# Delta net on unscaled queries and keys, decay sums spread by DMA, and two token chunks that enter the mixers with their norm's factor

## The chip, the core and the metric

The program runs on one core of a Trainium2 chip. A core has a matrix engine (TensorE, PE in the profile; PEld is its weight load), a vector engine (VectorE, DVE), a scalar engine (ScalarE, ACT), GpSimd (POOL) and SyncE (SP), whose queue issues nearly every DMA of this kernel. The metric is the device time of one execution in microseconds (us). Lines such as L1001 are lines of the kernel before, unless the text says that they belong to the changed one.

## The reference, cut to what matters

One decoder layer: a feed-forward block, two mixers side by side (windowed attention and a gated delta net), and a second feed-forward block. 1024 prompt tokens and 64 sample tokens (8 sequences of 8) go through it together. The change lies in the norm ahead of the mixers and in the delta net.

```python
h = rms_norm(x, mix_norm_pre)            # x * rsqrt(mean(x*x) + 1e-6) * gain
qa, ka, va, qkvb, zb, ab, bb, ga, gb = split_columns(h @ w_in)
xb = silu(causal_conv(qkvb));  qb, kb, vb = split(xb)
qb = l2_normalize(qb) * 128 ** -0.5      # x * rsqrt(sum(x*x) + 1e-6)
kb = l2_normalize(kb)
g = -exp(a_log) * softplus(ab + dt_bias);  beta = sigmoid(bb)
# per head and chunk of tokens, in float32
gc = cumsum(g);  decay = exp(gc_i - gc_j) for j <= i
m  = strict_lower(beta * (k @ k.T) * decay)
k_cum, v_u = solve(I + m, [beta * k * exp(gc), beta * v])
v_new = v_u - k_cum @ S
o     = (q * exp(gc)) @ S + ((q @ k.T) * decay) @ v_new
S     = S * exp(gc_last) + (k * exp(gc_last - gc)).T @ v_new
ob = rms_norm(o, dn_out_norm) * silu(zb)
merged = sigmoid(ga) * (oa @ w_branch_a) + sigmoid(gb) * (ob @ w_branch_b)
```

A query's length scales its whole row of `o`, and the norm on `o` takes it out again but for the small constant under the root. The final states do not depend on the queries.

## The kernel before

**Layout.** Features lie on the 128 partitions and tokens along the free axis. The 1088 tokens are three chunks, `CH` = 0 to 384, 384 to 768 and 768 to 1088. A weight or activation is kept as two tiles, a rounded one and the remainder (`split`, `split_w`), and each product is three matrix products with a rounded float32 type (L138 to L140 in `gemm`, L343 to L345 in the down projection, L462 to L464 in the up projection of chunks 0 and 1). Products of the delta net and the sums over partitions are plain float32; the profile holds two records for each such product.

**Stages.** The first feed-forward block ends with `close1(c)` for each chunk: `post` (norm of the output, residual), then `make_xn` (L198, L199), which multiplies by the gain alone and splits, and `rms`, which makes the row factor `r2[c]` from a sum over partitions (L175, a product with a matrix of ones). For chunks 0 and 1 these generators are stepped while the block's last passes run (`take(late, 3)`, L627). The mixers take `xn2`; since the factor is not in it, every product's result is multiplied by `r2[c]` as VectorE copies it out of PSUM (L666, L683, L694, L957, L1018, L1031). Those results rotate through three PSUM buffers, `pa`.

**Mixers.** Keys, values and queries of the attention, then 16 attention items, the sample attention, four delta heads, and as filler the products of the convolution inputs (`conv_unit`), the z gates (`z_unit`) and 16 gate units (`gate_unit`, L1021 on), which hang on nothing but `xn2` and weights.

**A delta head** (`delta_head`) works in eight slots of 128 x 1088 each; heads 0 and 2 use one set, 1 and 3 the other, and small PSUM tiles come from `ph` or `py`. `l2` normalizes q and k: square, sum over partitions by a product with ones (L1001), root on ScalarE (L1002, L1003), one Newton step (L145, L146), scaling (L1008). L1060 and L1099 make the rows of the cumulated decay, the same on all partitions, by a product of a broadcast column with a triangle. L1063 is k against q, L1066 the decay's exponent, L1076 the decay into q on POOL, L1080 a transpose, L1083 k against k, L1135 the transposes of k and v, L1141 to L1152 a forward substitution in blocks of 32, L1165 and L1166 the scaling of the inverse by the columns `bg` and `bh`, L1217 to L1236 the walk over the chunks. At the end `colsum_rsqrt` does the output's norm, and the gate z comes back by DMA (L1275).

**What sets the order.** A scheduler orders each engine's instructions before the run by its own cost model; the program's order and `high_priority` are its input. On the chip every engine's queue runs in that order.

Of the kernel before, what the change touches and what calls it, by code (L numbers as in the profile page):

```python
# [7 lines left out]
F32 = mybir.dt.float32  # L8
# [27 lines left out]
def body(ctx: ExitStack, tc: tile.TileContext, d):  # L36
# [25 lines left out]
    gd = dp.tile([16, P, NT], F32, tag="gd", name="gd")  # L62

# [468 lines left out]
    hn2 = cp.tile([P, KT], F32, tag="hn2", name="hn2")  # L532
    nc.vector.tensor_scalar_mul(hn1, vec[:, V_N1A : V_N1A + KT], -0.5)
# [14 lines left out]
    with tc.tile_pool(name="f1", bufs=12, side="left", reuse_waits="tile") as big1, tc.tile_pool(  # L548
# [78 lines left out]
        f1.run(xs1, cx1, lambda: again(d["x2"], hn1, r1[2]), before, lambda g, i: (g, i) != (CUT, 0) and take(late, 3), r=lambda g: None if g else r1[2], first=first)  # L627
# [26 lines left out]

    def do_ab(c):
        a, b = CH[c]
        n = b - a
        ps = pa()
        xh, xl = xn2[c]
        for k in range(KT):  # L660
            for j in (0, 1) if k < KT - 1 else (1, 0):
                m, x = ((16, xh), (8, xl))[j]
                nc.tensor.matmul(ps[:m, :n], wab[:, k, :m], at(x, k), start=k + j == 0, stop=k - j == KT - 1)
        ab = t1()
        with tc.high_priority(offset=20000):
            nc.vector.scalar_tensor_tensor(  # L666
                out=ab[:16, :n], in0=ps[:16, :n], scalar=-0.5, in1=r2[c][:16, :], op0=ALU.mult, op1=ALU.mult
            )
        pst = pb()
        for o in range(a, b, P):  # L670
            w = min(P, b - o)
            i = o // P
            tk2 = pst[:w, i * 16 : i * 16 + 16]
            nc.tensor.transpose(tk2, ab[:16, o - a : o - a + w], ident[:16, :16])
            nc.vector.tensor_copy(atok[:w, i, :], tk2[:, 0:8])
            nc.vector.tensor_tensor(out=atok[:w, i, :], in0=atok[:w, i, :], in1=tk2[:, 8:16], op=ALU.add)

    def do_kv(dst, w, c):
        a, b = CH[c]
        ps = pa()  # L680
        mm = gemm(ps, w, xn2, c)
        with tc.high_priority(offset=20000):
            nc.vector.scalar_tensor_tensor(  # L683
                out=dst[:, a:b], in0=ps[:, : b - a], scalar=-0.5, in1=r2[c], op0=ALU.mult, op1=ALU.mult
            )
        return mm

    def do_q(t, w, c):
        a, b = CH[c]
        ps = pa()  # L690
        mm = gemm(ps, w, xn2, c)
        e = min(b, NPR)
        with tc.high_priority(offset=20000):
            nc.vector.scalar_tensor_tensor(  # L694
                out=YA[t][:, a:e], in0=ps[:, : e - a], scalar=-0.0625, in1=r2[c][:, : e - a], op0=ALU.mult, op1=ALU.mult
            )
# [81 lines left out]
    nc.vector.tensor_tensor(out=tk["bg"], in0=tk["bg"], in1=tk["beta"], op=ALU.mult)  # L778

# [166 lines left out]
    def conv_unit(u, dst):  # L946
        w = unit(U_QKV + u, f"qkv{u}")
        cw = [vec[:, V_CW + u * 4 + j : V_CW + u * 4 + j + 1] for j in range(4)]
        for c, (a, b) in enumerate(CH):
# [6 lines left out]
            with tc.high_priority(offset=20000):  # L956
                nc.vector.scalar_tensor_tensor(  # L957
                    out=pre[:, 3 : 3 + m], in0=ps[:, :m], scalar=-0.5, in1=r2[c][:, :m], op0=ALU.mult, op1=ALU.mult
                )
# [37 lines left out]
    def colsum_rsqrt(src, sq, ve, rr, tmp, scale, ps):  # L997
        nc.scalar.activation(sq, src, AF.Square)
        for a, b in ((0, 512), (512, 1024), (1024, NT)):
            pq = ps()  # L1000
            nc.tensor.matmul(pq[:, : b - a], ones, sq[:, a:b], start=True, stop=True)  # L1001
            nc.scalar.activation(ve[:, a:b], pq[:, : b - a], AF.Identity, scale=scale, bias=epsc)  # L1002
        nc.scalar.activation(rr, ve, AF.Abs_reciprocal_sqrt)  # L1003
        newton(rr, ve, tmp)

    def l2(x, A, l2s, ps):
        colsum_rsqrt(x, A[4], A[3], A[5], A[4], 0.25, ps)
        nc.vector.scalar_tensor_tensor(out=x, in0=x, scalar=-0.25 * l2s, in1=A[5], op0=ALU.mult, op1=ALU.mult)  # L1008

    def z_unit(h):  # L1010
        w = unit(U_Z + h, f"z{h}")
        for c, (a, b) in enumerate(CH):
            n = b - a
            ps = pa()
            gemm(ps, w, xn2, c)
            z = t1()
            with tc.high_priority(offset=20000):
                nc.vector.scalar_tensor_tensor(out=z[:, :n], in0=ps[:, :n], scalar=-0.5, in1=r2[c], op0=ALU.mult, op1=ALU.mult)  # L1018
            sg = t3()
            nc.scalar.activation(sg[:, :n], z[:, :n], AF.Tanh, scale=0.5)  # L1020
            nc.vector.scalar_tensor_tensor(out=z[:, :n], in0=sg[:, :n], scalar=1.0, in1=z[:, :n], op0=ALU.add, op1=ALU.mult)  # L1021
            nc.sync.dma_start(zd[h, :, a:b], z[:, :n])

    def gate_do(i, w, c):
# [4 lines left out]
        z = t1()  # L1029
        with tc.high_priority(offset=20000):  # L1030
            nc.vector.scalar_tensor_tensor(out=z[:, :n], in0=ps[:, :n], scalar=-0.5, in1=r2[c], op0=ALU.mult, op1=ALU.mult)  # L1031
            nc.scalar.activation(z[:, :n], z[:, :n], AF.Tanh, scale=0.5)
# [7 lines left out]
    def delta_head(h, A, ps):  # L1040
        q, k, v, M, L, U, QK, R = A
        ar = R[:, :NPR].rearrange("p (i c) -> p i c", c=P)
        mq = s2b.tile([P, 2 * NSM], F32, tag="mq", name=f"mq{h}", bufs=2)

# [9 lines left out]
        D, E = R[:, 0:512], R[:, 512:1024]  # L1054
        for c0 in (0, 4):
            pr, pq = ps(), ps()
            for i in range(4):
                w, cs, ix = tile_of(c0 + i)
                ps_i = slice(i * P, i * P + P)
                nc.tensor.matmul(pr[:, ps_i], tk["g"][:, ix : ix + 1].to_broadcast([P, P]), cst[:, C_TRI : C_TRI + P], start=True, stop=True)  # L1060
            for i in range(4):
                w, cs, ix = tile_of(c0 + i)
                nc.tensor.matmul(pq[:, i * P : i * P + P], k[:, cs], q[:, cs], start=True, stop=True)  # L1063
            for i in range(4):
# [3 lines left out]
                    in0=pr[:, i * P : i * P + P],  # L1068
# [5 lines left out]
            nc.scalar.activation(E, pr, AF.Exp)  # L1074
# [6 lines left out]
            for i in range(4):  # L1081
                w, cs, ix = tile_of(c0 + i)
                nc.tensor.matmul(pk[:, i * P : i * P + P], k[:, cs], k[:, cs], start=True, stop=True)  # L1083
            nc.scalar.copy(D, pt)
            for i in range(4):
# [4 lines left out]
                    scalar=tk["beta"][:, ix : ix + 1],  # L1090
# [4 lines left out]
        for c in range(8, 9):  # L1095
            w, cs, ix = tile_of(c)
            tri, neg = cst[:w, C_TRIS : C_TRIS + w], cst[:w, C_NEGS : C_NEGS + w]
            p = ps()
            nc.tensor.matmul(p[:, 0:w], tk["g"][:w, ix : ix + 1].to_broadcast([w, P]), tri, start=True, stop=True)  # L1099
            nc.tensor.matmul(p[:w, 128 : 128 + w], k[:, cs], k[:, cs], start=True, stop=True)  # L1100
            nc.tensor.matmul(p[:w, 256 : 256 + w], k[:, cs], q[:, cs], start=True, stop=True)
            Ds = ar[:w, 0, :w]
            nc.vector.scalar_tensor_tensor(
                out=Ds, in0=p[:w, 0:w], scalar=tk["gc"][:w, ix : ix + 1], in1=neg, op0=ALU.subtract, op1=ALU.add
# [3 lines left out]
            nc.scalar.activation(eR, p[:, 0:w], AF.Exp)  # L1108
# [6 lines left out]
                out=M[:w, cs], in0=p[:w, 128 : 128 + w], scalar=tk["beta"][:w, ix : ix + 1], in1=DT, op0=ALU.mult, op1=ALU.mult  # L1115
# [15 lines left out]
        for c0 in (0, 4):  # L1131
            for t in (k, v):
                p = ps()
                for i in range(4):
                    nc.tensor.transpose(p[:, i * P : i * P + P], t[:, (c0 + i) * P : (c0 + i + 1) * P], ident)  # L1135
                nc.scalar.copy(wide(t, c0), p)
# [26 lines left out]
        def scale_u(c, Ub):  # L1163
            w, cs, ix = tile_of(c)
            nc.vector.tensor_scalar_mul(Ub, U[:w, cs], tk["bg"][:w, ix : ix + 1])  # L1165
            nc.scalar.mul(U[:w, cs], U[:w, cs], tk["bh"][:w, ix : ix + 1])  # L1166
# [35 lines left out]
        nc.tensor.transpose(p[:w, 0:128], k[:, cs], ident)  # L1202
        nc.tensor.transpose(p[:w, 128:256], v[:, cs], ident)
        nc.scalar.copy(ar[:w, 6:8, :], p[:w, 0:256].rearrange("p (i c) -> p i c", c=P))
# [3 lines left out]
        nc.tensor.matmul(p5[:, :w], ar[:w, 6, :], Ub, start=True, stop=True)  # L1208
# [51 lines left out]
        for hf in range(2):  # L1260
# [8 lines left out]
            nc.tensor.matmul(p6, ar[:NSM, 6, :], vm, start=True, stop=True)  # L1269
# [6 lines left out]
        colsum_rsqrt(QK, q, k, v, M, 1.0 / P, ps)  # L1276
# [230 lines left out]
```

## Time and profile before

| | us |
|---|---|
| median of 3 runs (2459.77 to 2460.8) | 2460.74 |
| the profiled execution | 2454.17 |
| its span, from the first to the last instruction | 2452.4 |
| PE busy in the span | 2396.3 |
| DVE busy | 1752.0 |
| ACT busy | 1146.2 |

The mean granted clock of TensorE was 0.991. The first feed-forward block runs to about 760 us, its end and the first mixer products lie between 760 and 800, attention from 858 to 985, the delta heads from about 985 to 1460, the last gates to 1490, and then the branch projections, the output projection and the second feed-forward block. A row of a view by line reads: line, engine, operation, tiles written and read, shape, count, then busy time in us, mean ns of one, and the engine's idle time just before them with what ended it. A row by stretch of time gives each engine's busy time in it, the count of instructions, the granted clock, the busy share of the DMA engines and GB/s.

### The profile page before, as it was taken

How to read it: one execution, taken by the hardware profiler on the slowest of the kernel's cores; microseconds unless marked ns; L12 is line 12 of the kernel's file. 1: busy time of each engine (PE TensorE's matmuls, PEld its weight loads, DVE VectorE, ACT ScalarE, POOL GpSimd, SP SyncE). 2: the span in 40 equal slices, each digit the busy share in tenths (PEclk: the TensorE clock that was granted, in tenths of full speed). 3: DMA queues.
4: the chain of work that ended last, by engine and by line, in shares of the span. 5: the costliest groups of instructions: out<-in, count | busy, mean ns of one | idle time of the engine just before them, and what ended most of it. 6: DMA issues, size and time to landing. Idle time of an engine off the chain costs nothing.

```text
span 2452.4 us, 39218 instructions
## 1 busy us (share of the span) xinstructions
PE 2396.3 (98%) x14654; PEld 2307.2 (94%) x14654; DVE 1752.0 (71%) x3550; ACT 1146.2 (47%) x2326; POOL 48.6 (2%) x36
## 2 busy tenths in 40 slices
PE   8999999999999999999999999999999999999997
PEld 7999999999998988798898889999999999999997
DVE  8887657757788577698796646655997576676677
ACT  7644423324465377644655333255754333233344
POOL 0000000000000000000101000000000000000000
PEclk9999999999999999999999999999999999999998
DMA  7332212213454301222222345435523122122453
GB/s 269 125 112 86 74 48 86 70 52 112 155 175 142 105 29 45 77 65 73 71 68 73 99 143 158 142 129 184 182 93 97 48 82 78 45 85 80 152 164 133
DMA packets 159759, 257.98 MB, mean 105 GB/s; under 512 B 34800, under 2 KB 65968, under 8 KB 159560
## 3 DMA queue, kind: packets, MB, share of 16 engines
q1 hardware_dynamic: 159568, 255.47, 32.4%
q8 instruction: 115, 1.88, 0.3%
q14 instruction: 76, 0.62, 0.1%
HBM read 219.43 MB, written 36.96 MB: 105 GB/s over the span
## 4 chain that ended last, share of the span: by engine, by line
PE 43%; DVE 6%; DMA 2%; ACT 1%; issue 1%; SPq 0%; DVEq 0%; ACTq 0%
PE pa L139 6%; PE pa L140 6%; PE pa L138 6%; PE pa L462 4%; PE pa L463 4%; PE pa L464 4%; PE py L344 2%; PE py L345 2%; PE ph L345 2%; PE ph L344 2%; PE ph L343 2%; PE py L343 2%; DMA q_c_a<-in_up_dram 1%; DVE s L1149 1%; DVE s L1143 1%
## 5 line engine op out<-in xcount | busy, mean ns | idle before, releaser
L463 PE MATMUL pa<-cl,h_c_s 128*128 128x384 f32 x704 | 236.4, 336 | 4.7 <-DVE cl L272 4.7
L462 PE MATMUL pa<-ch,h_c_s 128*128 128x384 f32 x704 | 237.4, 337 | 2.0 <-DVE t L468 1.4
L464 PE MATMUL pa<-ch,l_c_s 128*128 128x384 f32 x704 | 236.2, 336 | 0.0
L468 DVE TENSOR_TENSOR t<-pa,t 128x384 f32<-128x384 f32 x308 | 170.3, 554 | 83.6 <-PE pa L464 83.1
L462 PE MATMUL pa<-ch,h_c_a 128*128 128x384 f32 x528 | 176.8, 335 | 0.1
L464 PE MATMUL pa<-ch,l_c_a 128*128 128x384 f32 x528 | 176.6, 334 | 0.0
L463 PE MATMUL pa<-cl,h_c_a 128*128 128x384 f32 x528 | 176.5, 334 | 0.0
L111 ACT CAST h_c_a<-r_c_a 128x512 fp32r<-128x512 f32 x132 | 81.8, 619 | 129.8 <-PE pa L463 110.9
L462 PEld LDWEIGHTS pa<-ch,h_c_s 128*128 128x128 f32 x704 | 132.8, 189 | 5.6 <-DVE t L468 5.2
L463 PEld LDWEIGHTS pa<-cl,h_c_s 128*128 128x128 f32 x704 | 133.0, 189 | 4.9 <-DVE cl L272 4.9
L464 PEld LDWEIGHTS pa<-ch,l_c_s 128*128 128x128 f32 x704 | 132.9, 189 | 0.0
L111 ACT CAST h_c_s<-q_c_s 128x512 fp32r<-128x512 f32 x132 | 82.0, 621 | 107.1 <-PE pa L463 96.3
L139 PE MATMUL pa<-xbl,h_ga 128*128 128x384 f32 (+1 forms) x384 | 129.3, 337 | 0.0
L138 PE MATMUL pa<-xbh,h_ga 128*128 128x384 f32 (+1 forms) x384 | 128.7, 335 | 0.0
L140 PE MATMUL pa<-xbh,l_ga 128*128 128x384 f32 (+1 forms) x384 | 128.4, 334 | 0.0
L462 PEld LDWEIGHTS pa<-ch,h_c_a 128*128 128x128 f32 x528 | 99.1, 188 | 0.8 <-DVE t L468 0.6
L463 PEld LDWEIGHTS pa<-cl,h_c_a 128*128 128x128 f32 x528 | 99.1, 188 | 0.0
L464 PEld LDWEIGHTS pa<-ch,l_c_a 128*128 128x128 f32 x528 | 99.1, 188 | 0.0
L138 PE MATMUL pa<-xbh,h_qkv 128*128 128x384 f32 (+1 forms) x288 | 96.7, 336 | 0.0
L139 PE MATMUL pa<-xbl,h_qkv 128*128 128x384 f32 (+1 forms) x288 | 96.6, 335 | 0.0
L140 PE MATMUL pa<-xbh,l_qkv 128*128 128x384 f32 (+1 forms) x288 | 96.3, 334 | 0.0
L111 ACT CAST h_c_s<-r_c_s 128x512 fp32r<-128x512 f32 x44 | 27.4, 623 | 146.4 <-PE pa L463 130.6
(603 smaller groups left out, 7438.4 us busy)
## 6 DMA issues: line engine op xcount, KB each, us to landing
r_c_a<-in_up_dram SPq DMA_DIRECT2D x132, 256.0 KB
q_c_a<-in_up_dram SPq DMA_DIRECT2D x44, 256.0 KB
q_ub<-in_up_dram SPq DMA_DIRECT2D x44, 256.0 KB
r_ub<-in_up_dram SPq DMA_DIRECT2D x44, 256.0 KB
r_ua<-in_up_dram SPq DMA_DIRECT2D x42, 256.0 KB
q_ua<-in_up_dram SPq DMA_DIRECT2D x42, 256.0 KB
r_da<-in_dn_dram SPq DMA_DIRECT2D x40, 256.0 KB
q_da<-in_dn_dram SPq DMA_DIRECT2D x40, 256.0 KB
```

Source lines behind the costliest of these rows:

```text
L111: nc.scalar.copy(hi, full)
L138: nc.tensor.matmul(ps[:, :n], hi[:, j, :], at(xh, k), start=first, stop=False)
L139: nc.tensor.matmul(ps[:, :n], hi[:, j, :], at(xl, k), start=False, stop=False)
L140: mm = nc.tensor.matmul(ps[:, :n], lo[:, j, :], at(xh, k), start=False, stop=last)
L343: nc.tensor.matmul(ps[:, :n], hi[:, i, :], hh, start=i == 0, stop=False)
L344: nc.tensor.matmul(ps[:, :n], hi[:, i, :], hl, start=False, stop=False)
L345: nc.tensor.matmul(ps[:, :n], lo[:, i, :], hh, start=False, stop=i == len(hs) - 1)
L462: nc.tensor.matmul(ps, wh[:, k, :], xh[:, k, :], start=k == 0, stop=False)
L463: nc.tensor.matmul(ps, wh[:, k, :], xl[:, k, :], start=False, stop=False)
L464: nc.tensor.matmul(ps, wl[:, k, :], xh[:, k, :], start=False, stop=k == 3)
L468: nc.vector.tensor_tensor(out=out, in0=ps, in1=other, op=ALU.add)
L1143: nc.vector.tensor_tensor(out=tv, in0=Md[:, j + 1 :, j : j + 1].to_broadcast([34, m, j + 1]), in1=Ld[:, j : j + 1, 0 : j + 1].to_broadcast ...
```

## The change

1. **The norm's factor.** For chunks 0 and 1 `rms` comes before the split, and `make_xnr` multiplies gain and row factor into the activations (changed lines 213, then 193 and 194 for the split). Chunk 2 stays as it was. The mixers' results of chunks 0 and 1 are then copied out of PSUM by ScalarE (`normed`), or, in the gates, read from PSUM by the tanh itself; chunk 2 still goes through VectorE. The generators are stepped four at a time instead of three.
2. **Unscaled q and k.** `l2` is gone. The keys are transposed to token rows at the head's start (changed line 1075), the transposed rows are squared and summed along the free axis on ScalarE and VectorE, and the factor, now one number per token in a column, goes into `beta`, `bg` and `bh`. The queries stay as the convolution left them; their squares are kept in HBM (`sqd`) and added under the root of the output's norm.
3. **Decay sums.** One transpose of `gc` and nine small DMAs put the cumulated decay in HBM (`gcd`); each head reads its row back to all 128 partitions with one DMA into the slot of `QK`, in place of L1060 and L1099.

```diff
     def close1(c):
             ...
-            yield from make_xn(y, xn2[c], V_MXA)
+            r2[c] = rtile("r2", c)
             spill(y, xd[c])
-            r2[c] = rtile("r2", c)
-            yield from rms(big1, lambda k: at(y, k), width(c), r2[c], 1.0 / 1024.0)
+            if c == 2:
+                yield from make_xn(y, xn2[c], V_MXA)
+                yield from rms(big1, lambda k: at(y, k), width(c), r2[c], 1.0 / 1024.0)
+            else:
+                yield from rms(big1, lambda k: at(y, k), width(c), r2[c], 1.0 / 1024.0)
+                yield from make_xnr(y, xn2[c], hnx, r2[c], c)
...
-        ... and take(late, 3), r=lambda g: None if g else r1[2], first=first)
+        ... and take(late, 4), r=lambda g: None if g else r1[2], first=first)
...
+    def normed(out, ps, c, scale=1.0, p=P, o=0):
+        n = out.shape[-1]
+        with tc.high_priority(offset=20000):
+            if c < 2:
+                nc.scalar.mul(out, ps[:p, o : o + n], scale)
+            else:
+                nc.vector.scalar_tensor_tensor(
+                    out=out, in0=ps[:p, o : o + n], scalar=-0.5 * scale, in1=r2[c][:p, o : o + n], op0=ALU.mult, op1=ALU.mult
+                )
...
+    psc = pb()
+    nc.tensor.transpose(psc[:36, :P], tk["gc"], ident)
+    gct = s2b.tile([36, P], F32, tag="gct", name="gct")
+    nc.vector.tensor_copy(gct, psc[:36, :P])
+    for c in range(9):
+        nc.sync.dma_start(gcd[:, c, :], gct[4 * c : 4 * c + 4, :])
...
     def gate_do(i, w, c):
             ...
+        src = ps
+        if c == 2:
+            normed(z[:, :n], ps, c)
+            src = z
         with tc.high_priority(offset=20000):
-            nc.vector.scalar_tensor_tensor(out=z[:, :n], in0=ps[:, :n], scalar=-0.5, in1=r2[c], op0=ALU.mult, op1=ALU.mult)
-            nc.scalar.activation(z[:, :n], z[:, :n], AF.Tanh, scale=0.5)
+            nc.scalar.activation(z[:, :n], src[:, :n], AF.Tanh, scale=0.5)
...
     def delta_head(h, A, ps):
-        q, k, v, M, L, U, QK, R = A
+        q, kT_, v, M, k, U, QK, R = A
+        L = kT_
...
-        l2(q, A, P ** -0.5, ps)
-        l2(k, A, 1.0, ps)
+        nc.sync.dma_start(QK, gcd[h].rearrange("c t -> (c t)")[0:NT].unsqueeze(0).to_broadcast([P, NT]))
+        nk = s2b.tile([P, 5, 9], F32, tag="nk", name=f"nk{h}", bufs=2)
+        ss, rho, rho2, t9, bgr = (nk[:, i, :] for i in range(5))
+        nc.vector.memset(ss, 1.0)
+        for c0 in (0, 4, 8):
+            n = 4 if c0 < 8 else 1
+            w = P if c0 < 8 else NSM
+            pt = ps()
+            for i in range(n):
+                nc.tensor.transpose(pt[:w, i * P : i * P + P], kT_[:, (c0 + i) * P : (c0 + i) * P + w], ident)
+            nc.scalar.copy(wide(k, c0) if c0 < 8 else k8, pt[:w, : n * P])
+            nc.scalar.activation(M[:w, : n * P], pt[:w, : n * P], AF.Square)
+            nc.vector.tensor_reduce(out=ss[:w, c0 : c0 + n], in_=M[:w, : n * P].rearrange("p (i c) -> p i c", c=P), op=ALU.add, axis=AX.X)
+        nc.vector.tensor_scalar_add(ss, ss, 4.0 * EPS)
+        nc.scalar.activation(rho, ss, AF.Abs_reciprocal_sqrt)
+        newton(rho, ss, t9)
+        ...
+        nc.vector.tensor_tensor(out=bgr, in0=mine("bg"), in1=rho2, op=ALU.mult)
+        nc.vector.tensor_tensor(out=bhr, in0=mine("bh"), in1=rho, op=ALU.mult)
+        nc.vector.tensor_tensor(out=br2, in0=mine("beta"), in1=rho2, op=ALU.mult)
+        nc.scalar.activation(U, q, AF.Square, scale=P * EPS ** 0.5)
+        nc.sync.dma_start(sqd[h], U)
         for c0 in (0, 4):
-            pr, pq = ps(), ps()
+            pq = ps()
...
-                nc.tensor.matmul(pr[:, ps_i], tk["g"][:, ix : ix + 1].to_broadcast([P, P]), cst[:, C_TRI : C_TRI + P], start=True, stop=True)
...
-                    in0=pr[:, i * P : i * P + P],
+                    in0=QK[:, cs],
...
-            nc.scalar.activation(E, pr, AF.Exp)
+            nc.scalar.activation(E, wide(QK, c0), AF.Exp)
...
-            for t in (k, v):
-                p = ps()
-                for i in range(4):
-                    nc.tensor.transpose(p[:, i * P : i * P + P], t[:, (c0 + i) * P : (c0 + i + 1) * P], ident)
-                nc.scalar.copy(wide(t, c0), p)
+            p = ps()
+            for i in range(4):
+                nc.tensor.transpose(p[:, i * P : i * P + P], v[:, (c0 + i) * P : (c0 + i + 1) * P], ident)
+            nc.scalar.copy(wide(v, c0), p)
...
-        colsum_rsqrt(QK, q, k, v, M, 1.0 / P, ps)
+        nc.sync.dma_start(v, sqd[h])
+        nc.scalar.activation(q, QK, AF.Square)
+        nc.vector.tensor_tensor(out=q, in0=q, in1=v, op=ALU.add)
+        for a, b in ((0, 512), (512, 1024), (1024, NT)):
+            pq = ps()
+            nc.tensor.matmul(pq[:, : b - a], ones, q[:, a:b], start=True, stop=True)
+            nc.scalar.activation(k[:, a:b], pq[:, : b - a], AF.Identity, scale=1.0 / P, bias=eps4)
+        nc.scalar.activation(v, k, AF.Abs_reciprocal_sqrt)
+        newton(v, k, M)
```

**Two places in PE's order.** The first is where the first feed-forward block ends and the mixers begin. `pa` tiles take the mixers' products, `po` the sums over partitions (L175 before, L177 in the changed kernel), `kvq` and `k` are weights of the attention's projections, `xbh`/`xbl` the split activations. Before:

```order
L139 MATMUL pa_8407<-xbl_1_8038,h_k_8198 128x384
L140 MATMUL pa_8407<-xbh_1_8036,l_k_8199 128x384
L175 MATMUL po_8183<-rms_8170,eye_72 128x384
L175 MATMUL po_8220<-rms_8207,eye_72 128x320
L674 MATMUL py_8342<-eye_72,t_680_8340 128x16
L138 MATMUL pa_8445<-xbh_0_7313,h_kvq_0_0_8435 128x384
L139 MATMUL pa_8445<-xbl_0_7315,h_kvq_0_0_8435 128x384
```

The changed kernel, with chunk 2's sum for `post`:

```order
L142 MATMUL pa_8481<-xbh_1_7318,l_kvq_0_1_8478 128x384
L140 MATMUL pa_8481<-xbh_1_7318,h_kvq_0_1_8477 128x384
L177 MATMUL po_8256<-rms_8243,eye_72 128x320
L141 MATMUL pa_8481<-xbl_1_7320,h_kvq_0_1_8477 128x384
L142 MATMUL pa_8481<-xbh_1_7318,l_kvq_0_1_8478 128x384
L690 MATMUL py_8378<-eye_72,t_696_8376 128x16
L140 MATMUL pa_8507<-xbh_0_7895,h_kvq_0_0_8471 128x384
```

The two sums that stood together ahead of the first `kvq` products are apart: chunk 1's (128x384) has moved up into the feed-forward block's down projection, and chunk 2's (128x320) stands behind 22 products of a `kvq` weight.

The second place is the start of the fourth delta head among gate products (`ga`). Before, with the second of its two sums of squares and the first decay rows:

```order
L138 MATMUL pa_14346<-xbh_1_8244,h_ga_1_14284 128x320
L139 MATMUL pa_14346<-xbl_1_8246,h_ga_1_14284 128x320
L1001 MATMUL py_13746<-s_8300,eye_72 128x512
L1001 MATMUL py_13749<-s_8300,eye_72 128x512
L1001 MATMUL py_13752<-s_8300,eye_72 128x64
L140 MATMUL pa_14346<-xbh_1_8244,l_ga_1_14285 128x320
```

The changed kernel:

```order
L1075 MATMUL py_13732<-eye_72,s_8339 128x128 x4
L1075 MATMUL py_13740<-eye_72,s_8339 128x128 x4
L140 MATMUL pa_14172<-xbh_0_7317,h_ga_0_14162 128x384
L141 MATMUL pa_14172<-xbl_0_7319,h_ga_0_14162 128x384
L142 MATMUL pa_14172<-xbh_0_7317,l_ga_0_14163 128x384
L140 MATMUL pa_14172<-xbh_0_7317,h_ga_0_14162 128x384
L1075 MATMUL py_13748<-eye_72,s_8339 64x128
```

The head now begins with nine transposes of the keys in place of two sums of squares over 1088 columns, and no decay rows follow.

More of the change, by code (lines that the diff above doesn't have):

```diff
@@ L625, in before @@
                 drain(early)
-        f1.run(xs1, cx1, lambda: again(d["x2"], hn1, r1[2]), before, lambda g, i: (g, i) != (CUT, 0) and take(late, 3), r=lambda g: None if g else r1[2], first=first)
+        f1.run(xs1, cx1, lambda: again(d["x2"], hn1, r1[2]), before, lambda g, i: (g, i) != (CUT, 0) and take(late, 4), r=lambda g: None if g else r1[2], first=first)
         drain(late)
@@ L664, in do_ab @@
         ab = t1()
[L665 to L668, printed above, removed]
+        normed(ab[:16, :n], ps, c, p=16)
         pst = pb()
@@ L995, in conv_unit @@
             )
[L997 to L1008, printed above, removed]
+    eps4 = s2b.tile([P, 1], F32, tag="eps4", name="eps4")
+    nc.vector.memset(eps4, 4.0 * P * EPS * EPS)
     def z_unit(h):
```

64 lines of the change are left out of this document (31 added, 33 removed).

## The prediction

> **What bounds the kernel now.** I read the page's head first, for the engine that is never free:
>
> ```profile
> PE 2396.3 (98%) x14654; PEld 2307.2 (94%) x14654; DVE 1752.0 (71%) x3550; ACT 1146.2 (47%) x2326; POOL 48.6 (2%) x36
> PE 43%; DVE 6%; DMA 2%; ACT 1%; issue 1%; SPq 0%; DVEq 0%; ACTq 0%
> ```
>
> PE is busy 98% of the span and leads the chain of waits. A change gains what it takes off PE's queue, what idle time it removes there, and what half-clock time it removes. An edit on DVE or ACT counts only where PE waits for it.
>
> Next, the view by stretches of time, cut by stage. Its columns are start:end, length, then busy time (and count) of PE, PEld, DVE, ACT and POOL, granted clock, DMA share and GB/s:
>
> ```profile
> 774.00:779.00 5.00, 1.50 (x6) 0.57 (x4) 3.90 (x7) 3.58 (x8) 0.00 (x0) 0.97 0.30 95
> 779.00:786.00 7.00, 6.36 (x18) 4.92 (x19) 5.03 (x11) 2.62 (x7) 0.00 (x0) 0.54 0.02 7
> 858.00:985.00 127.00, 123.33 (x805) 103.16 (x806) 92.43 (x270) 98.89 (x307) 0.00 (x0) 1.00 0.13 40
> 985.00:1040.00 55.00, 50.73 (x357) 42.10 (x356) 36.46 (x102) 34.92 (x73) 5.23 (x4) 0.94 0.23 74
> 1040.00:1200.00 160.00, 156.10 (x1004) 142.15 (x1003) 139.82 (x379) 80.36 (x157) 15.19 (x10) 0.99 0.24 73
> 1200.00:1360.00 160.00, 156.87 (x1006) 141.58 (x1005) 123.62 (x335) 85.12 (x165) 18.95 (x13) 0.99 0.22 66
> 1460.00:1490.00 30.00, 30.00 (x190) 30.00 (x189) 15.81 (x31) 15.47 (x33) 0.00 (x0) 1.00 0.70 229
> ```
>
> Two places leave PE anything to win. At 774, where the feed-forward block ends, PE is idle 5.00 - 1.50 = 3.5 us, and then runs 7 us at a clock of 0.54. In the heads (985 to 1360) it is idle 4.3 + 3.9 + 3.1 = 11.3 us, though their own chain is long, because the gates fill it.
>
> **The change part by part: products removed.** The second sum of squares of the fourth head, between gate products, then a group of decay rows (the timeline of PE: start, length, instruction):
>
> ```profile
> 1296.55 2.34 PE L1001 MATMUL py<-s,eye 128*128 128x512 f32 x6 [1.81 <-ACT s L998]
> 1298.70 0.39 PE L140 MATMUL pa<-xbh,l_ga 128*128 128x320 f32 x1
> 1298.93 0.34 PE L138 MATMUL pa<-xbh,h_ga 128*128 128x384 f32 x1
> 1299.11 0.34 PE L139 MATMUL pa<-xbl,h_ga 128*128 128x384 f32 x1
> ...
> 1299.63 1.05 PE L1060 MATMUL py<-cst,tk_g 128*128 128x128 f32 x8
> 1300.44 0.42 PE L139 MATMUL pa<-xbl,h_ga 128*128 128x384 f32 x1
> ```
>
> Records overlap, so what a group takes from PE is the time from its start to the next start. One sum of squares (six records, three products): 1298.70 - 1296.55 = 2.15 us. Eight of the twelve go (two per head; the output norm's stay): 8 x 2.15 = 17.2. One group of L1060 (eight records, four products): 1300.44 - 1299.63 = 0.81; two per head go: 8 x 0.81 = 6.5. The single product of L1099 per head stands in the chain of waits, whose pieces do not overlap:
>
> ```profile
> 1225.76 0.36 PE ph L1099 x2
> ...
> 1230.08 0.86 PE py L1001 x2
> ...
> 1231.05 1.10 PE py L1001 x4
> ```
>
> It is 4 x 0.36 = 1.4. Sum 25.1. From below: the chain has a sum of squares at 0.86 + 1.10 = 1.96, so 8 x 0.19 less, 23.6. From above, the whole busy time of the groups by line and form:
>
> ```profile
> L1001 PE MATMUL py<-s,eye 128*128 128x512 f32 x24 | 12.7, 642 | 2.3 <-ACT s L998 2.2
> L1001 PE MATMUL ph<-s,eye 128*128 128x512 f32 x24 | 11.7, 596 | 0.7 <-ACT s L998 0.7
> L1001 PE MATMUL py<-s,eye 128*128 128x64 f32 x12 | 2.5, 288 | 1.3 <-ACT s L1002 1.3
> L1001 PE MATMUL ph<-s,eye 128*128 128x64 f32 x12 | 2.3, 274 | 0.0
> L1060 PE MATMUL ph<-cst,tk_g 128*128 128x128 f32 x32 | 5.2, 284 | 0.0
> L1060 PE MATMUL py<-cst,tk_g 128*128 128x128 f32 x32 | 4.4, 275 | 0.0
> ```
>
> 8/12 of 29.2 is 19.5, and 9.6 for L1060 with 1.4: 30.5, which counts the overlap twice. I take **25**, bounds 23 to 30. Nine key transposes per head are added at its start, and as many go at L1135 and L1202; one transpose of `gc` is new (about 0.1). Nothing there.
>
> **The boundary.** PE's timeline where the block ends:
>
> ```profile
> 777.56 0.91 PE L175 MATMUL po<-rms,eye 128*128 128x384 f32 x2 [2.97 <-DVE rms L171]
> 779.61 1.44 PE L175 MATMUL po<-rms,eye 128*128 128x320 f32 x2 [1.14 <-ACT rms L177]
> ```
>
> Both waits are for sums over partitions. In the changed order chunk 1's stands in the down projection and chunk 2's behind 22 products of a `kvq` weight (22 x 0.175 = 3.9 us: above, four products of 384 columns start between 1298.93 and 1299.63). So the idle 3.5 us and the half clock after it, (1 - 0.54) x 7.0 = 3.2, can go: up to 6.7. What is late next: chunk 1's split, since factor, multiplication and rounding now stand ahead of its first product. Those are 8 multiplications and 8 subtractions of 384 columns at about 0.55 (rows of L957 and L192 below) plus the Newton step, some 10 to 13 us of DVE, and four steps of the generators instead of three must bring them forward. I take **5**, bounds 0 (the split is as late as the sum was) to 7. By the Trainium skill, "TensorE: Matmul & The Clock Gate", section "What's actually happening", the clock halves after an idle window of about 3.4 us and needs about 3.4 us of work to return; by that rule a wait shorter than this loses no clock and the place gives 6.7. This case's trace agrees in kind (3.5 us idle, then 0.54).
>
> **Evictions and vector work.**
>
> ```profile
> L957 DVE SCALAR_TENSOR_TENSOR t<-pa,r 128x384 f32<-128x384 f32 x24 | 13.3, 552 | 17.5 <-PE pa L140 17.5
> L998 ACT ACTIVATE s<-s 128x1088 f32<-128x1088 f32 x12 | 13.3, 1108 | 11.0 <-DVE s L1256 5.7 <-DVE s L146 3.2 <-issue 2.1
> L1136 ACT COPY s<-py 128x512 f32<-128x512 f32 x8 | 4.6, 585 | 1.5 <-PE py L1135 1.4
> L192 DVE TENSOR_TENSOR ha<-t,ha 128x384 fp32r<-128x384 f32 x44 | 24.4, 554 | 2.1 <-ACT ha L191 1.3
> ```
>
> DVE loses 32 gate evictions outright and 46 others to ACT (78 x 0.55 = 43 us), and three passes of 1088 columns in each of 8 calls (24 x 1.28 = 31, the pass of L1008 further down); it gains 16 passes of 0.55 in the first block and small work. None of it is on PE's path, so I cost it at nothing. ACT loses 8 x 3 passes of 1.1 and gets 46 copies; a copy of 512 columns takes 0.58. What hides an ACT eviction is the three `pa` buffers: a tile's 24 products last 24 x 0.175 = 4.2 us, so it may be late by 8 us before PE waits. Without that cover, a copy behind a 1.11 us pass would cost 46 x 1.11 = 51; with ACT 78% busy in attention (98.89 of 127) this is unlikely.
>
> **The heads' chain.** The fourth head's key norm before, from its square to its scaling, on ACT and DVE:
>
> ```profile
> 1295.39 1.11 ACT L998 ACTIVATE s<-s 128x1088 f32<-128x1088 f32 x1 [0.33 <-DVE s L146]
> 1309.14 1.28 DVE L1008 SCALAR_TENSOR_TENSOR s<-s,s 128x1088 f32<-128x1088 f32 x1
> ```
>
> It takes 1310.4 - 1295.4 = 15 us, a query norm before it partly overlapped. Now two groups of four transposes, each with a copy and a square of 512 columns on ACT (0.58 each) and a reduction on DVE, then numbers of 128 x 9: some 5 us. So 10 us less per head, 40 in all; up to 60 with the query norm's unhidden part. This matters because the scheduler counted on it: 301 of the 1152 gate products stood behind the last head's output sum, now 454 do. The heads run with 153 fewer filler products, 153 x 0.175 = 27 us less cover, and 25 us fewer products of their own, so the phase is meant to be 52 us shorter. Where the chain shortens by 40, PE waits up to 12 us more; where by 60, none. Against that go the waits ahead of L1001, 2.3 + 0.7 + 1.3 = 4.3 for twelve calls, 8/12 of them or 2.9. I take **+1** for the two together, bounds +3 and -9.
>
> **Decay rows.** The nearest transfer is z's read of 544 KB into a slot, issued at 1148.21; the stretches around it:
>
> ```profile
> 1148.20:1149.10 0.90, 0.90 (x6) 0.84 (x7) 0.00 (x0) 0.32 (x2) 0.90 (x1) 1.00 0.00 0
> 1149.10:1151.30 2.20, 2.20 (x12) 1.64 (x11) 1.96 (x6) 0.69 (x2) 0.76 (x1) 1.00 0.73 253
> ```
>
> It moves for 2.2 us and has landed 1151.3 - 1148.2 = 3.1 us after its issue. A broadcast has the same bytes to write and is issued at the head's start, ahead of the 5 us of key work, which hides it; cover gone, 3.1 per head, 12 in all. The queue can take the cover away: the slot's last reader on POOL holds the SP queue, in which the broadcast stands behind it.
>
> ```profile
> SPq L1279 <- POOL s L1278: 19.4, 4, 8.8
> ```
>
> SP waits there up to 8.8 us already. The queries' squares (a write and a read per head) go into stretches with a DMA share near 0.24 and are needed only at the head's end. Nothing, bound 12.
>
> **Sum:** 25 + 5 + 1 = 31. The profiled execution took 2454.17, 6.6 below the median of the runs. It becomes 2423, and the median 2460.7 - 31 = **2430**.
>
> **The rivals.**
>
> A. *The boundary gives nothing, and the heads wait.* Chunk 1's split is as late as its sum was (boundary 0) and the chain's shortening leaves 5 us of new waits (between +1 and -9): 25 + 0 - 5 = 20, **2440**. For it: DVE is busy 3.90 of 5.00 at 774. Against: four steps instead of three.
>
> B. *Decay rows late* at each head, 12 us: -31 + 12, **2442**. For it: the 8.8 us wait on POOL in that queue. Against: the first use comes after key work.
>
> C. *The clock falls at the heads' starts.* A stretch with PE busy throughout, but with small products of the heads, and the one behind it:
>
> ```profile
> 1342.00:1345.00 3.00, 3.00 (x25) 2.80 (x23) 1.57 (x5) 0.44 (x3) 0.86 (x1) 1.00 0.24 77
> 1345.30:1348.70 3.40, 3.40 (x11) 2.46 (x9) 2.62 (x7) 1.29 (x2) 0.74 (x1) 0.50 0.73 240
> ```
>
> The clock halves for 3.4 us although PE is never idle, a loss of 1.7. If each of the four runs of key transposes does this, 4 x 1.7 = 7 comes back: **2437**. Against: gate products stand between the groups. The Trainium skill ("TensorE: Matmul & The Clock Gate", "Part 4: PE-mode transpose") says that transposes do not count as PE work for the clock, which speaks for C; no row of before has a run of transposes alone to test it.
>
> D. *The heads lack filler*: **slower**. The order is fixed, so the 454 gate products cannot come forward on the chip. If the chain shortens by x and not by 52, PE waits 52 - x; against the 30 of the other terms that is no gain at x = 22 (5.5 us per head), and slower below. At x = 10 the change is -30 + 42 = +12, **2473**. For it: DVE is 87% busy from 1040 to 1200, and the chain might be set there and not by the norm. Against: DVE loses 31 us of passes in the heads, and most of its gate evictions.
>
> E. *More*: the idle 11.3 us and half-clock time of the heads (0.94 over 55 us, 0.99 over 320: 6.5 us) mostly go too, 14 on top: **2416**.
>
> **How the numbers follow.** Forecast 0.48 (alone 2424 to 2436), A 0.20, B 0.08, C 0.09, E 0.05; D 0.10, half of it slower and half at no gain. The range 2418 to 2447 holds the forecast, C, B and most of A, and leaves out D, E and a tail of A, under 0.2. A change of 0.2%, 4.9 us, is about what a measurement of this kernel can tell from none. Faster 0.90, within 0.2% 0.05, slower 0.05.
>
> **What would show it.** PE's busy time falls by about 25 in the heads, with its waits there near 11 us as before: the products' term. More than 20 us of waits there, mostly on ACT and DVE of a head's start, is D; waits of the decay exponent's DVE pass for a DMA are B; half clock after the transposes is C. At the boundary the two waits for sums are gone and no wait for the split of chunk 1 has come: the 5 us. DVE's busy time falls by some 60 and PE does not wait for ACT's evictions. After about 1450 the stages keep their lengths. The forecast is wrong if a wait that I cost at nothing, above all on the broadcast or the split, holds PE.

## The result, and the profile after

| | before | the change |
|---|---|---|
| median of 4 runs, us | 2460.26 (2457.51 to 2460.8) | 2434.86 (2431.4 to 2440.89) |
| ratio, with its 95% interval | | 0.9902 (0.988 to 0.9923) |
| the profiled execution, us | 2454.17 | 2440.89 |
| its span, us | 2452.4 | 2439.1 |

The change is faster by 24 us (19 to 30). The forecast of 2430 was 5 us low, and its range held the time. The profiled execution of the change is the longest of its four runs, and that of before is shorter than the median of its runs, so the two traces differ by 13 us only; the section on the hardware comes back to what separates runs of one kernel. All medians are of executions in the usual state; one execution of the run e8 below took 5965 us and is left out.

The row of busy times from the head of the page after:

```profile
PE 2373.7 (97%) x14535; PEld 2291.1 (94%) x14535; DVE 1704.9 (70%) x3519; ACT 1127.3 (46%) x2344; POOL 50.9 (2%) x36
```

PE has 119 records fewer and is 22.6 us less busy; DVE is 47 us less busy, where the prediction had some 60. The view by stretches, for the same stages as before, and the whole mixers behind the boundary in one row:

```profile
700.00:760.00 60.00, 59.08 (x392) 57.48 (x391) 52.51 (x101) 41.29 (x81) 0.00 (x0) 1.00 0.50 167
760.00:800.00 40.00, 38.41 (x218) 33.78 (x217) 33.44 (x67) 23.89 (x52) 0.00 (x0) 1.00 0.38 124
985.00:1040.00 55.00, 51.48 (x379) 45.76 (x378) 40.22 (x142) 32.40 (x81) 5.34 (x4) 0.94 0.38 115
1040.00:1200.00 160.00, 149.21 (x973) 135.56 (x971) 124.12 (x374) 75.57 (x172) 22.58 (x14) 0.96 0.25 77
1200.00:1360.00 160.00, 153.57 (x957) 141.03 (x955) 122.23 (x327) 68.25 (x139) 18.37 (x12) 0.98 0.31 98
858.00:1490.00 632.00, 608.17 (x3912) 549.05 (x3911) 421.20 (x1192) 329.24 (x816) 50.74 (x32) 0.98 0.29 93
```

The same last row of the kernel before:

```profile
858.00:1490.00 632.00, 614.86 (x3970) 548.74 (x3971) 460.43 (x1219) 349.86 (x809) 48.42 (x32) 0.99 0.25 78
```

The boundary is as forecast: from 760 to 800 the clock is whole and PE idle 1.6 us instead of 4.1. In 700 to 760 PE now waits 0.9 us, which it did not. The heads are not as forecast: from 858 to 1490 PE is idle 23.8 us instead of 17.1, at a clock of 0.98 instead of 0.99. This is the kernel's and not one execution's: the profile of e9, the change run again, has PE busy for the same time there within 0.5 us, and the same two waits on the decay's exponent (7.2 us, the longest 4.9).

```profile
858.00:1490.00 632.00, 607.69 (x3899) 547.95 (x3899) 419.57 (x1191) 328.83 (x817) 50.83 (x32) 0.98 0.29 92
```

The largest waits of PE in that stretch (us in total, times, longest), changed kernel:

```profile
PE py L1119 <- ACT s L1114: 7.1, 2, 4.7
PE py L1215 <- ACT s L1212: 3.2, 1, 3.2
PE py L1211 <- DMA s<-bd: 2.6, 1, 2.6
PE ph L883 <- ACT s L832: 2.5, 6, 0.6
```

L1114 is the decay's exponent, L1119 its transpose, L1212 the copy of a product of the substitution, L832 an exponential of the attention. Both waits on the exponent are in the second head. What ACT did there:

```profile
1051.65 0.63 ACT L1113 ACTIVATE s<-s 128x512 f32<-128x512 f32 x1 [1.82 <-POOL s L1115]
1052.30 1.28 ACT L1082 ACT_TABLE_LOAD   x1
...
1054.06 1.28 ACT L1114 ACT_TABLE_LOAD   x1
1055.35 0.63 ACT L1114 ACTIVATE s<-s 128x512 f32<-128x512 f32 x1
...
1064.25 0.63 ACT L1114 ACTIVATE s<-s 128x512 f32<-128x512 f32 x1 [2.38 <-DVE s L1105]
```

Both wait for a pass of DVE (L1105), whose parts DVE did between steps of the head before's substitution. For the first exponent the last part ended at 1054.00, and then stood the second of two table loads of 1.28 us ahead of it (the first is for the key factor's root); for the second the last part ended at 1064.2.

### The profile page after: what moved, and what is told of

The parts are those of the page before. It is cut to its first block, busy times and chain, and to the rows that moved or that the text cites. A ratio compares the mean times of both kernels' runs of the same rounds, so it can differ in the third digit from the quotient of the medians.

```text
span 2439.1 us, 38987 instructions
## 1 busy us (share of the span) xinstructions
PE 2373.7 (97%) x14535; PEld 2291.1 (94%) x14535; DVE 1704.9 (70%) x3519; ACT 1127.3 (46%) x2344; POOL 50.9 (2%) x36
## 4 chain that ended last, share of the span: by engine, by line
PE 48%; DVE 6%; DMA 1%; ACT 1%; issue 1%; SPq 0%; POOL 0%; DVEq 0%; ACTq 0%; POOLq 0%
PE pa L140 7%; PE pa L142 7%; PE pa L141 7%; PE pa L464 4%; PE pa L465 4%; PE pa L466 4%; PE ph L346 2%; PE ph L347 2%; PE py L347 2%; PE py L346 2%; PE py L345 2%; PE ph L345 2%; DVE s L1186 1%; DVE s L1180 1%; DVE t L980 1%
```

## The experiments

Ratios are to the kernel before, run beside each on one chip; 0.001 is 2.5 us. Runs e1 to e4, e5 to e8 and e9 to e12 are three sets, each on its own chip, so what is compared across sets is ratios and not times. The change alone had 0.9902, and in a later repetition (e9) 0.9911.

**The parts apart.** Part 1 alone on the kernel before, then parts 2 and 3 alone:

```diff
# e1: kernel before with close1, take(late, 4) and normed() of the change, delta_head of before
# e2: kernel before with delta_head, gcd and sqd of the change, norm of before
```

> The kernel before with part 1 alone (norm factor in chunks 0 and 1, ScalarE evictions, four generator steps). Theory: only the boundary gains, the idle 3.5 us and most of the half clock after it, so 4 to 6 us below the kernel before, about 2455, and heads as before. Rival (vector relief or ScalarE evictions matter): a gain of 10 or more by fewer waits in the heads, or a loss with waits of the products on ScalarE's evictions.

> The kernel before with parts 2 and 3 alone (unscaled keys and queries, decay rows by DMA). Theory: 25 us of products go and 5 to 10 come back as waits and half clock at the heads' decay exponents, so 15 to 20 below, about 2442, with the boundary as before. Rival (the parts lean on each other, VectorE being needed by both): under 12 us of gain alone, or norm part and delta part together well short of, or beyond, the whole change's 25.

e1: 2459.0, ratio 1.0012 (0.9992 to 1.0033). No gain. e2: 2442.1, ratio 0.9934 (0.9909 to 0.9959), 16 us. Their sum, 13 us (about 5 to 21), is short of the change's 24 (19 to 30), though the intervals meet. In e1's trace the boundary row is the change's (clock 1.00, PE busy 38.41), and the rest gives it back:

```profile
760.00:800.00 40.00, 38.41 (x219) 33.78 (x218) 33.46 (x68) 25.39 (x56) 0.00 (x0) 1.00 0.36 119
...
858.00:1490.00 632.00, 611.36 (x3917) 543.62 (x3917) 422.91 (x1142) 357.61 (x830) 48.94 (x32) 0.98 0.25 76
```

PE is idle 20.6 us there, 3.5 more than before, at the lower clock, with the same products. So part 1 brings something in that belongs to neither the boundary nor the delta net.

**Who evicts.** The suspicion was the order of the engines: the 46 copies out of PSUM went from DVE to ACT.

```diff
             if c < 2:
-                nc.scalar.mul(out, ps[:p, o : o + n], scale)
+                nc.vector.tensor_scalar_mul(out, ps[:p, o : o + n], scale)
```

> The changed kernel with the 46 results of chunks 0 and 1 copied out of PSUM by VectorE (a plain scaling) instead of ScalarE. Theory (the norm part gains nothing alone because ScalarE evicts late, and pays in the whole change because VectorE is relieved): 3 to 6 us more than the changed kernel, about 2440. Rival (the evictor does not matter): within 2 us of the changed kernel.

> The kernel before with part 1 alone, evictions on VectorE. With evictions on ScalarE part 1 alone gained nothing. Theory (ScalarE, still loaded with the key and query norms, evicts late in the heads): 3 to 5 us below the kernel before, about 2453, the boundary's gain. Rival (the gain is lost ahead of the boundary, where chunk 1's sum of squares now holds the down projection and the split's passes come): no gain again, about 2458.

e6 (in the whole change): 2428.3, ratio 0.9873 (0.9855 to 0.9891), 3 to 4 thousandths below the change, where I had expected the opposite sign. e7 (part 1 alone): 2454.1, ratio 0.9986 (0.997 to 1.0002), below e1 by 2.6 thousandths. The intervals of these pairs overlap at their ends; a third pair (e5 and e10 below) has the same sign, by 1.3, with intervals that overlap for the most part. As medians the three pairs put 3 to 9 us on ScalarE's evictions. The clock blurs them: with the time that it lost taken off, as the last section does, all ten runs of e7 lie below all ten of e1 (7.6 us on average), and all four of e10 below all four of e5 (6.2), while e6 is 2 us below the change. So that the evictor matters is shown; how much in the whole change is not. With VectorE's evictions the boundary's gain stays: about 3 us alone. The waits of PE from 858 to 1490 in e6:

```profile
PE py L1119 <- ACT s L1114: 3.9, 1, 3.9
PE py L1075 <- DVE s L1008: 3.8, 3, 2.4
PE py L1211 <- DMA s<-bd: 3.0, 1, 3.0
PE ph L1075 <- DVE s L1008: 2.4, 2, 1.9
PE ph L883 <- ACT s L832: 2.0, 5, 0.7
...
PE pa L140 <- DVE t L668: 0.9, 1, 0.9
```

The direct wait for an evicted tile (L668) is small, 0.9 here and 1.3 in the change. What goes is waits on other work of ACT's queue (the wait for L1212 is gone, that for L1114 is 3.9 instead of 7.1), and waits on the convolution (L1008) take a part of their place. From 858 to 1490 PE is idle 21.0 us at 0.99:

```profile
858.00:1490.00 632.00, 610.96 (x3954) 549.96 (x3953) 434.37 (x1223) 315.28 (x779) 49.44 (x32) 0.99 0.30 94
```

That a copy on ACT delays the next one behind it is what these waits fit. The scheduler's order changes with the evictor too, and no run holds that order fixed, so the share of each is open.

**Three steps or four.**

```diff
-        ... and take(late, 4) ...
+        ... and take(late, 3) ...
```

> The changed kernel with the generators stepped three at a time instead of four. Theory (four steps are what bring chunk 1's factor and split forward): the boundary waits again, 4 to 7 us more than the changed kernel, about 2440, with the wait between 765 and 790. Rival (three are enough): within 2 us of the changed kernel, and the wait of the down projection for chunk 1's sum of squares near 705 smaller.

e8: 2444.4, ratio 0.9942 (0.9922 to 0.9961), some 8 to 10 us more than the change. The boundary, and its first `wab` product, which now reads activations with the factor in them:

```profile
760.00:800.00 40.00, 32.40 (x164) 26.68 (x162) 33.07 (x64) 24.07 (x51) 0.00 (x0) 0.91 0.30 106
```

```profile
768.12 0.91 PE L177 MATMUL po<-rms,eye 128*128 128x384 f32 x2 [1.40 <-DVE rms L173]
774.28 0.50 PE L682 MATMUL pa<-xbh,wab 128*16 128x384 f32 x1 [5.25 <-ACT xbh L193]
```

This is what the prediction called late next, chunk 1's split: a 5.25 us wait, and the half clock with it. The fourth step is what takes it away.

**Products put back.** Two runs ask what a removed product was worth: in e3 the two sums of squares per head run again on PE and nobody reads them; in e5 the decay rows are products again.

```diff
# e3
+        for _ in range(2):
+            for a, b in ((0, 512), (512, 1024), (1024, NT)):
+                nc.tensor.matmul(ps()[:, : b - a], ones, q[:, a:b], start=True, stop=True)
# e5
-        nc.sync.dma_start(QK, gcd[h] ... .to_broadcast([P, NT]))
+            nc.tensor.matmul(pr[...], tk["g"][...].to_broadcast([P, P]), cst[:, C_TRI ...])
```

> The changed kernel with the two sums of squares per head put back as bare PE products (24 products whose results nobody reads), nothing else undone. Theory (each PE product costs its time even though the heads now wait): 8 x 2.15 = 17 us more than the changed kernel, about 2452. Rival (the removed products had become filler for waits): under 8 us more, about 2440, the waits of the exponents shrinking by what is put back.

> The changed kernel with part 3 undone: the decay rows by products of TensorE again (L1060's and L1099's kind), no broadcast. Theory (each product costs its time): 6.5 + 1.4 = 8 us more than the changed kernel, about 2443. Rival (the DMA rows make the heads wait, or the products were filler): within 3 us of the changed kernel or below it, about 2435.

e3: 2448.1, ratio 0.9953 (0.9938 to 0.9968), 10 to 13 us more than the change for 17 us of products. e5: 2436.3, ratio 0.9903 (0.9886 to 0.992): the same as the change, for 8 us of products. So the rows by DMA bring nothing that the medians can tell. The trace of e5 shows who paid for its products:

```profile
PE py L1065 <- DVE s L999: 6.8, 3, 3.5
PE ph L874 <- ACT s L823: 3.4, 6, 0.9
PE py L1205 <- DMA s<-bd: 2.7, 1, 2.7
...
858.00:1490.00 632.00, 612.50 (x3990) 555.00 (x3990) 420.68 (x1186) 325.77 (x807) 48.90 (x32) 0.99 0.29 89
```

The waits on the exponent are gone, a wait on the keys' convolution has come, and PE is idle 19.5 us instead of 23.8, at 0.99 instead of 0.98: 4 us of idle time and some 6 us of clock (0.01 of 632) against 8 us of products. The clock's part is not one execution's: e5's four runs had 0.993 to 0.994, the change's eight 0.988 to 0.992. With the lost clock taken off, e5 is 6 us above the change and e3 14. So most of a product's length was time; without it PE waits more often, and the clock takes the gain back.

**Taking the exponents' waits away.** Each group of four chunks gets its own place for the exponent.

```diff
-        D, E = R[:, 0:512], R[:, 512:1024]
         for c0 in (0, 4):
+            D, E = wide(M, c0), wide(R, c0)
```

> The changed kernel with a place of its own for each group's decay exponent and row exponential (D in the slot of M, E over both halves of R), so that the second group of four chunks does not wait for the first one's last reader. Theory (the 7.1 us that PE waits for the exponents in the second head come from that one buffer, and the half clock behind them follows): 4 to 9 us below the changed kernel, about 2428, the second wait of 4.7 gone. Rival (the exponents are late because VectorE interleaves another head's substitution): within 2 us of the changed kernel, the waits in the same places.

e4: 2435.9, ratio 0.9912 (0.9888 to 0.9935): no difference. The second wait on the exponent is gone and PE is idle as long as before it, since other waits came:

```profile
PE pa L140 <- ACT t L668: 2.9, 2, 2.5
PE py L937 <- ACT s L832: 2.8, 2, 1.7
PE py L1120 <- ACT s L1115: 2.7, 1, 2.7
...
858.00:1490.00 632.00, 608.53 (x3918) 547.66 (x3917) 419.49 (x1192) 327.55 (x812) 47.28 (x32) 0.98 0.30 93
```

The one buffer held up an exponent, but taking it away gave no time that can be told; my theory of it fell.

**Looking for a better version.** On VectorE evictions: rows by products (e10), the keys' convolution first (e11), and that with the exponents' own places (e12); e9 is the change again.

```diff
# e11, e12
-        for j in range(3):
+        for j in (1, 0, 2):
             conv_unit(4 * j + h, A[j])
```

> The changed kernel unaltered, beside the next three on one chip, to place them against it. Both theories: 24 us below the kernel before, give or take 4, about 2434.

> VectorE evictions, and the decay rows by TensorE's products. With ScalarE evictions the products put back cost nothing. Theory (the heads' chain, not the evictor, hides them: PE waits there for a head's start and exponents either way): within 3 us of the change with VectorE evictions, about 2429. Rival (they were hidden by waits that ScalarE's evictions made): the full 8 us more, about 2437.

> VectorE evictions, and the keys' convolution ahead of the queries' in each head, since the key transposes now begin a head and PE waited 6.2 us for the last step of that convolution (five waits). Theory: that wait falls to 2 or less and the time by 2 to 6 us from 2428, to about 2424. Rival (the scheduler's order of the filler decides, and the wait moves to the exponents): within 2 us of 2428, the waits on the exponents larger.

> As the one before, and with a place of its own for each group's exponent. Theory: the exponents' wait of 3.9 us goes too, 2 to 4 us below keys first alone, about 2421. Rival (as when tried on the changed kernel, where its own place gave nothing): within 2 us of keys first alone.

| | median us | ratio |
|---|---|---|
| e9, the change again | 2437.3 | 0.9911 (0.9891 to 0.9932) |
| e10, VectorE, rows by products | 2431.8 | 0.989 (0.9874 to 0.9906) |
| e11, VectorE, keys first | 2432.6 | 0.9895 (0.9875 to 0.9914) |
| e12, VectorE, keys first, own places | 2436.4 | 0.9914 (0.9893 to 0.9935) |
| e6, VectorE (earlier, another set of runs) | 2428.3 | 0.9873 (0.9855 to 0.9891) |

None is below e6. e10 is 4 us above it with an interval of some 6 either way, so whether the rows by DMA are worth their 8 us there stays open. In e11 the waits on the convolution fell from 6.2 to 2.7 us (rows L1075 <- DVE L1008, one of them not shown), and the head start's squares and the exponents took it over:

```profile
PE py L1119 <- ACT s L1114: 3.7, 4, 1.5
PE py L1075 <- ACT s L1077: 3.1, 1, 3.1
PE py L1211 <- DMA s<-bd: 2.5, 1, 2.5
PE ph L1075 <- DVE s L1008: 2.2, 1, 2.2
```

The lowest is e6, the change with VectorE's evictions. It is clear of the kernel before; against the change the intervals meet, and of e10 to e12, with the same evictor, two lie between these and one beside the change.

## Why the prediction was right, and where its steps were not

**Products, 25 us.** As work they are right: with each product counted at the usual step of its shape, from start to start, the trace after has 24.0 us less. As time they were not all worth their length: 10 to 13 of the sums' 17 (e3), and none of the rows' 8 that the medians could tell (e5). The step that failed is "A change gains what it takes off PE's queue", where the heads stand: there a product also fills a wait and keeps the clock up, and the prediction gave its length alone.

**The boundary, 5 us.** Right at its place: 2.5 us of idle time and 3.4 us of clock (6.8 us at half) gone, 0.9 us back ahead of it. The late split was named as the risk, and e8 shows it, 5.25 us, as soon as the generators take three steps.

**Evictions at nothing.** This step was wrong. Three `pa` buffers do hide the eviction from the product that wants the buffer, as the prediction said (1.3 us of waits on L668 in the heads). But ACT's queue runs in order, and what PE waits for on ACT is seldom the eviction: it is the exponent, the copies of the substitution, the attention's exponentials. The pairs of runs put 3 to 9 us on the evictor; that it acts through ACT's queue is what the waits fit, and not shown apart from the scheduler's new order.

**The heads' chain, +1 (bounds +3 to -9).** The last head's output sum comes 39 us earlier (the last record of L1001 starts at 1439.1, in the changed kernel that of L1317 at 1399.8), and some of this is the boundary's; the prediction had the scheduler count on 52 for the heads. PE pays the rest: 6.7 us more idle time from 858 to 1490 in the profile after, 7.2 in e9's. The clock takes 6.9 and 8.6 us more there in these two profiles (27 and 31 us at half clock instead of 14), but both are of executions with a low clock (0.989; the change's runs have 0.991 on average, as those of before). So in the mean it takes less, by an estimate about the 3.4 us that the boundary gave. That makes the term some -10 in place of +1, just beyond the lower bound and in the direction of rival D, short of its 20 us of waits.

**The sum.** With these, 24 + 5 - 10 = 19, against 24 (19 to 30) measured and 31 forecast. The forecast was too high by the heads' term, in which the evictions' price is counted too; that it came out within 7 us is in part luck, since some 5 us of the measured gain have no place in this account. With VectorE's evictions the change gives 31 us (27 to 36), the forecast's own size, which may be chance, since e6's trace also has more idle time in the heads than before (21.0 against 17.1).

**The rivals.** A's number, 2440, rested on the boundary giving nothing, which it did not. B (rows late) shows in the first head, at a fraction of its 12 us. Its row landed 4.9 us after its issue at 987.77, where the prediction had 3.1, and DVE's queue stood still for it with steps of the attention behind it. PE then waited for the attention's exponential, ahead of which ACT also had a table load, so how much of this wait is the row's is open:

```profile
992.68 0.35 DVE L1105 SCALAR_TENSOR_TENSOR s<-s,tk_gc,cst 128x128 f32<-128x128 f32 x1 [1.26 <-DMA s<-gcd]
996.48 0.33 PE L937 MATMUL py<-eye,s 128*128 128x128 f32 x1 [1.36 <-ACT s L832]
```

ACT waited for the row 2.2 us in two heads, this one included. PE's two long waits on the exponent are not for it: they stood behind VectorE's queue and a table load. C (half clock after the transposes) shows in another form: the half clock comes back at the heads' places where PE waits, below. D was the right worry at a third of its size.

**Open.** Why the two parts together give more than their sum: 24 against 13, where the intervals meet, and 31 against 16 + 3 with VectorE's evictions. With the lost clock taken off it is 23 against 14, but 24 against 21 with VectorE's evictions, so most of it goes with the evictor. The scheduler writes a new order for each, and no run here separates that from VectorE's relief.

## What to carry to other kernels

Price an eviction by what stands behind it in its engine's queue, and not only by the buffers that hide it from its own product: moving 46 copies to the less busy engine cost time here, and the waits fit that this engine also did what the long chain waits for. Where a stage lives on filler, a product taken out of it is worth its length only as long as no wait, and no half clock behind a wait, takes the place; one run with the products put back, unread, tells how much. And removing one wait (e4, e11) gave no time that could be told, as other waits came in its place.

## What the runs showed of the hardware

**The clock is lost after short waits.** Six times in the heads of the changed kernel the granted clock fell to half; each time PE had been idle for a part of the stretch just before. Four of them, the stretch and the one behind it:

```profile
1053.30:1056.10 2.80, 0.45 (x4) 0.13 (x3) 2.64 (x10) 2.61 (x5) 0.00 (x0) 1.00 0.00 0
1056.10:1059.50 3.40, 3.40 (x16) 3.24 (x17) 2.40 (x12) 0.58 (x1) 0.00 (x0) 0.50 0.02 5
1154.20:1158.50 4.30, 1.07 (x9) 0.80 (x8) 3.81 (x17) 2.57 (x7) 0.00 (x0) 1.00 0.39 123
1158.50:1161.90 3.40, 3.40 (x21) 3.12 (x19) 2.50 (x5) 1.22 (x3) 0.00 (x0) 0.50 1.01 388
1256.80:1260.90 4.10, 1.38 (x9) 0.82 (x6) 4.10 (x13) 3.35 (x7) 0.00 (x0) 1.00 0.29 45
1260.90:1264.30 3.40, 3.19 (x14) 3.19 (x14) 3.40 (x10) 2.36 (x6) 0.00 (x0) 0.50 0.52 149
1349.10:1353.00 3.90, 1.30 (x12) 1.01 (x10) 0.00 (x0) 0.00 (x0) 0.00 (x0) 1.00 0.45 110
1353.00:1356.50 3.50, 3.50 (x17) 3.50 (x16) 0.21 (x1) 1.08 (x2) 0.00 (x0) 0.51 0.68 228
```

Idle times of 2.4, 3.2, 2.7 and 2.6 us, not all in one piece, each cost 1.7 us more at half clock, so these waits cost 1.5 to 1.7 times their length. At the other two places (998.1 and 1062.9) the half clock lasts 6.8 us, behind 1.4 and 2.7 us of idle time. Key transposes alone did not do it: in three of the four heads no such stretch begins within 8 us of them. The Trainium skill ("TensorE: Matmul & The Clock Gate", section "What's actually happening") lets the clock fall after a whole idle window of about 3.4 us; here shorter waits with some products among them were enough.

**And after narrow products.** Waits are not the only cause: before, the stretch from 1345.3 that the prediction shows came with PE busy throughout. So do stretches from 1120.0 and 1307.7 in e9 and from 1387.7 in e6. Each of the four has, in the 3.4 us ahead of it, the 16 records of the sample tokens' products with 16 columns (L1282, before L1246). One of them, in e9:

```profile
1117.52 1.90 PE L1282 MATMUL ph<-mq,s 128*128 128x16 f32 x16
1116.60:1120.00 3.40, 3.40 (x28) 3.27 (x28) 2.43 (x6) 0.96 (x4) 0.44 (x1) 1.00 0.56 180
1120.00:1123.40 3.40, 3.40 (x14) 2.85 (x13) 1.21 (x3) 1.39 (x4) 1.45 (x1) 0.50 0.71 228
```

A busy PE in the profile is thus not always one that keeps its clock. These products alone do not decide it: the profile after has four such groups too, and no half clock right behind any. The same program lost its clock at other places in e9 than in the profile after, and no run shows what decides.

**Runs of one kernel differ by their clock.** The 19 runs of the kernel before beside e1 to e4 took 2452 to 2471 us at granted clocks of 0.995 to 0.986. Take from each the time that the clock lost, (1 - clock) times its span, and 2434 to 2440 is left, with an average of 2436.5; for the change's four runs it is 2412 to 2417. On that count the change gives 23 us. The two profiled executions, counted alike, stand 18 apart and not 13. The averages of the other runs, by the same count: e1 2440, e2 2419, e3 2427, e4 2416, e5 2420, e6 2411, e7 2432, e8 2418, e9 (the change again) 2413, e10 2414, e11 2412, e12 2411; the kernel before beside them has 2436 to 2437 on all three chips. The count sharpens a comparison of orders, and is not the time: a kernel that makes PE wait also lowers its clock, and pays for it.
